# The 32x32 blocks of the delta rule's inverses: from ScalarE's copies to transfers within SBUF, and the decay bias moved into the exponential

## The chip, the cores and the metric

The kernel runs on one core of a Trainium2 chip. The metric is the device time of one execution in microseconds (us). Before the change it is 2154.05 us, the median of three runs (2153.97 to 2155.12). A core has five engines, each with an instruction queue of its own that is worked off in order: TensorE (PE, with weight loads listed as PEld), VectorE (DVE), ScalarE (ACT), GpSimd (POOL) and SyncE (SP), which in this kernel issues all DMA transfers.

## The reference, cut to what matters

One encoder layer: RMSNorm, one large input projection, a convolution branch, a gated delta-rule branch (8 heads, two directions), a merge, an output projection, a SwiGLU feed-forward layer and a per-layer embedding. Only the delta rule is touched. For each chunk of 64 positions and each head and direction it solves a unit lower triangular system:

```python
g = jnp.cumsum(g, axis=-1)
decay = jnp.exp(jnp.where(tri_incl, g[..., :, None] - g[..., None, :], -jnp.inf))
lower = jnp.where(tri_strict, jnp.einsum('bhncd,bhnsd->bhncs', k_beta, k) * decay, 0.0)
sol = lax.linalg.triangular_solve(lower, rhs, left_side=True, lower=True, unit_diagonal=True)
```

## The kernel before, in words

Everything is float32. The large products are made of three passes each (`mm3`: high times high, high times low, low times high, with parts rounded by ACT's cast and DVE's subtraction in `split`); their matmuls read 128x512 columns and appear in the profile as `ps<-big,w`. Below they are called fill, since they are what TensorE does beside the delta rule. The fill of the first half of the program is the input projection's columns, the gates, the embedding's projection and the convolution's output product.

The delta rule runs per group of two heads (`group(g)`, four groups), and in a group per head (`head(...)`). In `group`, section `d.np`, the decay matrix of a head is built for eight blocks of 128 positions: two rows of cumulated logs are broadcast from DRAM into `rf` and `rb`, each block gets its bias from `gneg`, a minimum picks the direction, and ACT takes the exponential. In section `d.inv` the 32x32 diagonal blocks of both heads (two directions, eight blocks of 128 with four 32-blocks each) are inverted together on DVE; the result is the tile `v`. In `head`, section `d.lev`, two transposes on DVE bring `v` into the tiles `rr` and `rt`; then for each half `q4` of the head two tiles `eu` and `et` (four blocks, two directions, 128x128 each) are filled with zeros by GpSimd, and sixteen 32x(4x32) pieces are copied onto their diagonals. Two levels of small float32 matmuls follow, each with a negation on ACT (`neg`) between its two products, which join 32-blocks to 64 and 64 to 128. After that come the values (`d.v`), the chain over the eight blocks in both directions (`d.chain`) and the output (`d.out`).

No order is written out by hand. The program is recorded as a list of operations (`Plan.add`), each with an engine, a cost and its buffers, and `Plan.order` puts them in order by a simulated run: each engine takes the ready operation of the lowest level (the delta rule -1.8, weight loads -3.0, fill 0.5 to 2.7) at the simulated time. The constants that the change touches belong to these costs (`SWITCH`, `DMA_LAT`, `DMA_RATE`, the extra cost in `act` and in `square_transpose`). So any change of a cost can move instructions everywhere in the program. The order on each engine is then fixed; on the chip each engine's queue waits at its head for semaphores. The tiles of the delta rule come from eleven buffers of line `d`; a raw weight block has four buffers, split weights six. All instructions are issued from helpers: L239 is a matmul, L244 a transpose on TensorE, L263 a plain copy or cast on ACT, L270 any other ACT function, L286 a DVE operation, L319 a zero fill, L335 a DMA.

Of the kernel before, what the change touches and what calls it, by code (L numbers as in the profile page):

```python
# [15 lines left out]
AF = mybir.ActivationFunctionType  # L16
# [124 lines left out]


TABLES = {AF.Exp: 0, AF.Sigmoid: 1, AF.Silu: 2, AF.Ln: 3}
SWITCH = 1.31
AGE = 4

COLD = 25.0

DMA_LAT, DMA_RATE = 1.6, 300000.0
HOLD = {"dve": 0.24, "act": 0, "pe": 0}  # L150


# [22 lines left out]
class Plan:  # L175
# [70 lines left out]
    def act(self, out, in_, func=AF.Copy, scale=1.0, bias=None, accum=None):  # L246
        cost = (0.051 if in_.buf.pool.space == PSUM else 0.093) + in_.n / 1200
        outs, ins, kw = [out], [in_], {}
        if isinstance(scale, View):
            ins.append(scale)  # L250
            cost += 0.093
        if isinstance(bias, View):
            ins.append(bias)
            cost += 0.093
        if accum is not None:
            outs.append(accum)
            cost += 0.125 if in_.buf.pool.space == PSUM else 0.1
        if out.p1 - out.p0 < P and out.buf.tag == "big" and out.n <= 256:
            cost += 0.125

        def go():
            if func == AF.Copy and accum is None and not isinstance(scale, View) and scale == 1.0:
                return self.nc.scalar.copy(out.ap(), in_.ap())  # L263
            if isinstance(scale, View) or scale != 1.0:
                kw["scale"] = scale.ap() if isinstance(scale, View) else scale
            if bias is not None:
                kw["bias"] = bias.ap() if isinstance(bias, View) else bias
            if accum is not None:
                kw["accum_out"] = accum.ap()
            return self.nc.scalar.activation(out.ap(), in_.ap(), func, **kw)  # L270

        self.add("act", go, outs, ins, cost, table=TABLES.get(func))
# [32 lines left out]

    def square_transpose(self, out, in_):
        self._vec("transpose", "dve", dict(out=out, in_=in_))
        self.ops[-1].cost += 0.14

    def recip(self, out, in_):  # L310
        self.add("dve", lambda: self.nc.vector.reciprocal(out=out.ap(), in_=in_.ap()), [out], [in_],
# [28 lines left out]
    def order(self):  # L340
# [59 lines left out]
        while len(done) < total:  # L400
# [65 lines left out]
            if e == "sp":  # L466
                free[e] = now + o.cost
                begin = max(dma_free, now + DMA_LAT)
                dma_free = begin + o.nbytes / DMA_RATE
                o.end = dma_free  # L470
            else:
                free[e] = o.end = now + o.cost
# [65 lines left out]
P = 128  # L538
# [17 lines left out]
def hs(h):  # L556
    return slice(h * HW, (h + 1) * HW)


def cs(j):  # L560
    return slice(j * P, (j + 1) * P)
# [45 lines left out]
def hybrid_block(tc, x, p, g_mix, w_in, conv_dw_w, conv_dw_b,  # L607
# [25 lines left out]
    def bank():  # L633
        return ps_.tile([P, HW], tag="ps", line="any", cap=bank_cap[0])
# [13 lines left out]
    def const(name, shape):  # L648
        return cp.tile(shape, tag=name)
# [23 lines left out]
    beta = const("beta", [P, 16, NJ])  # L673
    gdec = const("gdec", [P, 16, NJ])
    gneg = const("gneg", [P, 16, NJ])
    e_g = const("e_g", [P, 16, NJ])
    e_ng = const("e_ng", [P, 16, NJ])
    e_t = const("e_t", [P, 16, NJ])
# [154 lines left out]
    def logits():  # L833
        to(LV["logits"], "logits")
        wr = medium([P, KB, 32], line="wab")
        w2 = medium([P, KB, 64], F32R, line="wab2")
        pn.dma(wr, w_in[0, :, C_AB:C_AB + 32].rearrange("(k q) c -> q k c", q=P))
        split(w2[:, :, 0:32], w2[:, :, 32:64], wr)
        lg = large([64, T], line="lg")
        for h in range(2):  # L840
            ps = bank()[:64]
            for k in range(KB):
                for i in range(2):
                    pn.matmul(ps, w2[:, k], hT[i][k][:, hs(h)], k == 0 and i == 0, k == KB - 1 and i == 1)
            pn.act(lg[:, hs(h)], ps)
        ps = bank()
        for j in range(NJ):
            pn.matmul(ps[:, j * 32:(j + 1) * 32], lg[:, cs(j)], ident2, True, True)
        psv = ps[:, :NJ * 32].fold(NJ, 32).perm(1, 0)
        bc = tin.tile([P, 2, 16], tag="bc", bufs=1)  # L850
        pn.dma(bc[:, 0], a_log[0].rearrange("d h -> (d h)").partition_broadcast(P))
        pn.dma(bc[:, 1], dt_bias[0].rearrange("d h -> (d h)").partition_broadcast(P))
        g4 = medium([P, 4, 16, NJ], line="g4")
        ga, gu, ge, gl = [g4[:, i] for i in range(4)]
        pn.act(beta, psv[:, 16:32], AF.Sigmoid)
        pn.tt(ga, psv[:, 0:16], bc[:, 1, :, None].spread(16, NJ), ALU.add)
        pn.act(ge, ga, AF.Abs)
        pn.act(ge, ge, AF.Exp, scale=-1.0)
        pn.act(bc[:, 0], bc[:, 0], AF.Exp)

        pn.ts(gu, ge, 1.0, ALU.add)
        pn.act(gl, gu, AF.Ln)
        pn.stt(ge, gu, -1.0, ge, ALU.add, ALU.subtract)
        pn.recip(gu, gu)
        pn.tt(ge, ge, gu, ALU.mult)
        pn.tt(gl, gl, ge, ALU.subtract)
        pn.stt(gl, ga, 0.0, gl, ALU.max, ALU.add)
        pn.stt(gdec, gl, -1.0, bc[:, 0, :, None].spread(16, NJ), ALU.mult, ALU.mult)
        for dst, mf, mb in ((e_g, m_le, m_ge), (e_t, m_gt, m_lt), (e_l, ones, ones)):
            ps = bank()  # L870
            pn.matmul(ps[:, 0:64], mf, gdec[:, 0:8], True, True)
            pn.matmul(ps[:, 64:128], mb, gdec[:, 8:16], True, True)
            pn.act(dst, ps[:, :128].fold(16, NJ), AF.Exp)
            if dst is e_g:
                pn.act(gneg, ps[:, :128].fold(16, NJ), AF.Copy, scale=-1.0)
        pn.ts(e_ng, e_g, -1.0, ALU.mult)
        ps = bank()
        pn.transpose(ps[:, :P], gneg.at(0, [(1, P)]), ident)
        gr = medium([P, P], line="gr")
        pn.act(gr, ps[:, :P], AF.Copy, scale=-1.0)  # L880
        pn.dma(d_g, gr)
# [136 lines left out]
    def group(g):  # L1018
# [6 lines left out]
        for hh in range(2):  # L1025
# [23 lines left out]

            rf, rb = decay_row(hd), decay_row(8 + hd)  # L1050
            for j in range(NJ):
                pn.act(rf[:, cs(j)], rf[:, cs(j)], AF.Identity, bias=gneg[:, hd, j:j + 1])
            for j in range(NJ):
                pn.stt(rf[:, cs(j)], rb[:, cs(j)], gneg[:, 8 + hd, j:j + 1], rf[:, cs(j)], ALU.add, ALU.min)
            for q4 in range(2):
                ps = bank()
                for i in range(4):
# [2 lines left out]
                    pn.act(ps[:, cs(i)], ps[:, cs(i)], AF.Square, accum=ssq[:, hh, j:j + 1])  # L1060
            pn.ts(ssq[:, hh], ssq[:, hh], EPS, ALU.add)
            dec = rf
            for q4 in range(2):
                pn.act(dec[:, hs(q4)], dec[:, hs(q4)], AF.Exp)

            nt = slot([P, NJ, P])
            for q4 in range(2):
# [57 lines left out]
    def head(g, hh, v, N, kT, nrm, b_, zt, ssq):  # L1125
        hd = 2 * g + hh

        pn.sec = "d.lev"
        rr, rt = slot([P, 32, 2, 16]), slot([P, 32, 2, 16])
        pn.square_transpose(rr.at(0, [(32, 32), (1, 32)]), v)  # L1130
        pn.square_transpose(rt.at(0, [(32, 32), (1, 32)]), v.perm(1, 0))
        U = []
        for q4 in range(2):
            eu, et = slot([P, 4, 2, P]), slot([P, 4, 2, P])
            pn.fill(eu, 0.0)
            pn.fill(et, 0.0)
            u0 = hh * 8 + q4 * 4
            for r in range(4):
                q = slice(32 * r, 32 * r + 32)

                pn.act(eu[q, :, 0, q], rt[q].at(16 + u0, [(1, 4), (32, 32)]))
                pn.act(eu[q, :, 1, q], rr[q].at(u0, [(1, 4), (32, 32)]))
                pn.act(et[q, :, 0, q], rt[q].at(u0, [(1, 4), (32, 32)]))
                pn.act(et[q, :, 1, q], rr[q].at(16 + u0, [(1, 4), (32, 32)]))
            nt = N[:, q4 * 4:q4 * 4 + 4]
            ps = bank()
            for u in range(4):
                pn.matmul(ps[:, cs(u)], nt[:, u], pair32(et, u), True, True)

            w1 = neg(ps)  # L1150
            px = bank()
            for u in range(4):
                pn.matmul(px[:, cs(u)], w1[:, u], pair32(eu, u), True, True)

            for c in range(4):
                q, r = slice(32 * (c ^ 1), 32 * (c ^ 1) + 32), slice(32 * c, 32 * c + 32)
                pn.act(eu[q, :, c % 2, r], px[q].fold(4, P)[:, :, r])
            pn.square_transpose(et[32:64, :, 0, 0:32], eu[0:32, :, 1, 32:64])
            pn.square_transpose(et[64:96, :, 1, 96:128], eu[96:128, :, 0, 64:96])
            ps = bank()  # L1160
            for u in range(4):
                pn.matmul(ps[:, cs(u)], nt[:, u], pair64(et, u), True, True)
            w2 = neg(ps)
            px = bank()
            for u in range(4):
                pn.matmul(px[:, cs(u)], w2[:, u], pair64(eu, u), True, True)
            for c in range(2):
                q, r = slice(64 * (1 - c), 64 * (1 - c) + 64), slice(64 * c, 64 * c + 64)
                pn.act(eu[q, :, c, r], px[q].fold(4, P)[:, :, r])
            U.append(eu)  # L1170
# [602 lines left out]
```

## Time and profile before

| | |
|---|---|
| median of 3 runs | 2154.05 us |
| the profiled execution | 2155.1 us |
| its span, first to last instruction | 2153.4 us |
| mean granted TensorE clock | 0.992 |
| DMA issues on SP | 1003 |

The span has four stretches: a start up to 200 us, the delta rule with fill from about 200 to 1050 us, the passage to the output products from 1050 to 1300 us, and large products from there to the end. A row of the view by windows gives, for each stretch, the busy time of each engine with the number of instructions in brackets, then the granted TensorE clock, the mean share of the DMA engines and GB/s. A row of the groups gives line, engine, operation, output<-input, shape, count, busy time and mean duration in ns, and the idle time just before. A row of the view of waits says which engine waited for which operation: total, times, longest.

### The profile page before, as it was taken

The numbers are of one execution on the slowest core, as the hardware profiler recorded it, in microseconds if no ns is written. First come the engines' busy times: TensorE is split into PE (matmuls) and PEld (weight loads), VectorE is DVE, ScalarE is ACT, GpSimd is POOL, SyncE is SP. The second block draws the span as 40 slices with busy tenths as digits, with TensorE's granted clock in tenths as the row PEclk, the third lists the DMA queues.
The fourth block names the chain that finished last, engine by engine and source line by source line (L and its number), as shares of the span: only waits on it lengthen the run. The fifth ranks groups of instructions, "written<-read, shape, count | busy, mean of one in ns | idle before, by whom it ended". The sixth has DMA issues, their size and how long they took to land.

```text
span 2153.4 us, 29679 instructions
## 1 busy us (share of the span) xinstructions
PE 2102.0 (98%) x10434; PEld 1733.1 (80%) x10434; DVE 1602.6 (74%) x2621; ACT 1082.5 (50%) x2495; POOL 129.1 (6%) x203
## 2 busy tenths in 40 slices
PE   7999999999999999999999999999999999999998
PEld 5888788878888888888887788888888888888888
DVE  4478989869799899986846877886666667452676
ACT  6725665856675666479644344533333334121542
POOL 1000110012010110101000000000000000000000
PEclk9999999999999999999999999999999999999999
DMA  6333323522442324435567587332222228221253
GB/s 212 119 102 119 123 74 102 189 83 84 133 152 74 128 103 142 142 115 174 174 212 222 189 265 245 103 97 84 74 83 83 84 72 279 66 94 38 66 166 110
DMA packets 289077, 278.69 MB, mean 129 GB/s; under 512 B 17209, under 2 KB 217074, under 8 KB 288928
## 3 DMA queue, kind: packets, MB, share of 16 engines
q1 hardware_dynamic: 288928, 276.79, 40.2%
q8 instruction: 82, 1.34, 0.3%
q14 instruction: 67, 0.55, 0.1%
HBM read 198.02 MB, written 78.71 MB: 129 GB/s over the span
## 4 chain that ended last, share of the span: by engine, by line
PE 52%; DVE 3%; ACT 2%; issue 1%; DMA 0%; SPq 0%; DVEq 0%; POOLq 0%; POOL 0%; ACTq 0%
PE ps L239 52%; DVE big L286 2%; ACT big L263 1%; DVE mid L286 1%; DVE w L286 0%; PE ps L244 0%; DMA mid<-d 0%; ACT mid L270 0%; ACT big L270 0%; ACT m L270 0%; ACT mid L263 0%; ACT w L263 0%; SPq L335 0%; ACT z L270 0%; DVE lnb L286 0%
## 5 line engine op out<-in xcount | busy, mean ns | idle before, releaser
L239 PE MATMUL ps<-big,w 128*128 128x512 f32 (+1 forms) x7524 | 1841.4, 399 | 7.4 <-DVE w L286 5.8
L239 PEld LDWEIGHTS ps<-big,w 128*128 128x128 f32 x7524 | 1384.6, 189 | 315.8 <-DVE w L286 7.9
L286 DVE SCALAR_TENSOR_TENSOR big<-big,cw 128x1024 f32<-128x1024 f32 x336 | 433.3, 1295 | 16.4 <-ACT big L270 10.3
L263 ACT CAST w<-raw 128x512 fp32r<-128x512 f32 (+2 forms) x340 | 199.6, 590 | 367.2 <-PE ps L239 282.5
L286 DVE TENSOR_TENSOR w<-raw,w 128x512 fp32r<-128x512 f32 (+2 forms) x340 | 223.2, 662 | 114.0 <-ACT w L263 108.1
L263 ACT CAST w<-mid 128x512 fp32r<-128x512 f32 x125 | 77.4, 621 | 155.7 <-PE ps L239 129.3
L286 DVE TENSOR_TENSOR big<-ps,big 128x512 f32<-128x512 f32 (+1 forms) x132 | 89.7, 686 | 83.1 <-PE ps L239 75.9
L286 DVE TENSOR_TENSOR w<-mid,w 128x512 fp32r<-128x512 f32 x125 | 85.7, 687 | 79.8 <-ACT w L263 79.6
L286 DVE TENSOR_TENSOR big<-big 128x512 fp32r<-128x512 f32 (+2 forms) x159 | 107.4, 708 | 10.6 <-ACT big L263 10.2
L239 PE MATMUL ps<-big 128*128 128x128 f32 (+1 forms) x784 | 105.6, 282 | 8.7 <-ACT big L263 6.2
L239 PEld LDWEIGHTS ps<-big 128*128 128x128 f32 x784 | 100.0, 193 | 17.4 <-issue 9.2
L263 ACT COPY big<-big 32x128 f32<-32x128 f32 (+1 forms) x264 | 102.4, 441 | 15.5 <-DVE big L286 9.1
L263 ACT COPY big<-ps 32x128 f32<-32x128 f32 (+3 forms) x162 | 66.6, 412 | 71.9 <-PE ps L239 65.9
L263 ACT CAST big<-big 128x512 fp32r<-128x512 f32 x120 | 71.2, 619 | 44.3 <-DVE big L286 23.1
L244 PE MATMUL ps<-ident,big 128*128 128x128 f32 (+2 forms) x432 | 73.8, 286 | 10.4 <-DMA big<-in_x_dram 8.1
L270 ACT ACTIVATE mid<-mid 128x512 f32<-128x512 f32 (+2 forms) x87 | 50.6, 590 | 59.3 <-DMA mid<-d 31.0
L239 PEld LDWEIGHTS ps<-S,big 128*128 128x128 f32 x448 | 69.3, 190 | 13.0 <-DVE S L286 1.7
L239 PE MATMUL ps<-S,big 128*128 128x128 f32 x448 | 74.2, 276 | 2.0 <-DVE S L286 1.7
L239 PEld LDWEIGHTS ps<-big,m 128*128 128x128 f32 x512 | 63.8, 196 | 14.0 <-ACT m L270 12.0
L244 PEld LDWEIGHTS ps<-ident,big 128*128 128x128 f32 (+2 forms) x432 | 55.1, 149 | 22.7 <-issue 10.5
L239 PE MATMUL ps<-big,m 128*128 128x128 f32 x512 | 67.6, 283 | 4.6 <-ACT m L270 4.4
L270 ACT ACTIVATE big<-big 128x1024 f32<-128x1024 f32 (+2 forms) x80 | 56.8, 714 | 28.9 <-DVE big L286 24.1
(158 smaller groups left out, 1697.2 us busy)
## 6 DMA issues: line engine op xcount, KB each, us to landing
d<-mid SPq DMA_DIRECT2D x162, 256.0 KB, 2.3
raw<-in_w_in_dram SPq DMA_DIRECT2D x128, 256.0 KB, 3.1
mid<-d SPq DMA_DIRECT2D x120, 256.0 KB, 3.1
big<-d SPq DMA_DIRECT2D x92, 256.0 KB, 5.0
big<-dqkv SPq DMA_DIRECT2D x32, 512.0 KB, 4.1
raw<-in_w_gate_up_dram SPq DMA_DIRECT2D x50, 256.0 KB, 2.9
dqkv<-big SPq DMA_DIRECT2D x24, 512.0 KB, 2.6
mid<-in_w_gate_up_dram SPq DMA_DIRECT2D x46, 256.0 KB, 3.8
```

Of the source, the lines that this page charges most:

```text
L239: o = self.add("pe", lambda: self.nc.tensor.matmul(out.ap(), lhsT.ap(), rhs.ap(), start=start, stop=stop), [out], [lhsT, rhs], cost)
L244: self.add("pe", lambda: self.nc.tensor.transpose(out.ap(), in_.ap(), ident.ap()), [out], [in_, ident], 0.110)
L263: return self.nc.scalar.copy(out.ap(), in_.ap())
L270: return self.nc.scalar.activation(out.ap(), in_.ap(), func, **kw)
L286: return getattr(e, name)(**{k: v.ap() if isinstance(v, View) else v for k, v in kw.items()})
```

## The change

Three things change in what is computed where, and four planner costs with them.

1. In `d.lev` the sixteen ACT copies per half head become sixteen DMAs from `rr` and `rt` to `et` and `eu` (256 in all, 16 KB each); those of `et` now stand ahead of those of `eu`. For the source of each to be contiguous, `rr` and `rt` are laid out as (unit, column) and the two transposes write with a stride of 32 elements.
2. In `d.np` ACT's eight additions of `gneg` to `rf` per head go. The minimum uses the difference `gdif` of both directions' biases, computed once, and the forward bias is added inside the exponential, which is now eight ACT instructions of 128 columns per head instead of two of 512.
3. Planner: a table switch costs 1.41 instead of 1.31, a DMA holds the simulated transfer line at least 0.3, a short copy costs 0.025 more, a large square transpose 0.36 more.

```diff
-SWITCH = 1.31
+SWITCH = 1.41
...
-DMA_LAT, DMA_RATE = 1.6, 300000.0
+DMA_LAT, DMA_RATE, DMA_MIN = 1.6, 300000.0, 0.3
...
-            cost += 0.125
+            cost += 0.15
...
-        self.ops[-1].cost += 0.14
+        self.ops[-1].cost += 0.14 if out.n < T else 0.5
...
-                dma_free = begin + o.nbytes / DMA_RATE
+                dma_free = begin + max(o.nbytes / DMA_RATE, DMA_MIN)
...
+    gdif = const("gdif", [P, NH, NJ])
...
+        pn.tt(gdif, gneg[:, NH:], gneg[:, :NH], ALU.subtract)
...
-                pn.act(rf[:, cs(j)], rf[:, cs(j)], AF.Identity, bias=gneg[:, hd, j:j + 1])
-            for j in range(NJ):
-                pn.stt(rf[:, cs(j)], rb[:, cs(j)], gneg[:, 8 + hd, j:j + 1], rf[:, cs(j)], ALU.add, ALU.min)
+                pn.stt(rf[:, cs(j)], rb[:, cs(j)], gdif[:, hd, j:j + 1], rf[:, cs(j)], ALU.add, ALU.min)
...
-            for q4 in range(2):
-                pn.act(dec[:, hs(q4)], dec[:, hs(q4)], AF.Exp)
+            for j in range(NJ):
+                pn.act(dec[:, cs(j)], dec[:, cs(j)], AF.Exp, bias=gneg[:, hd, j:j + 1])
...
-        rr, rt = slot([P, 32, 2, 16]), slot([P, 32, 2, 16])
-        pn.square_transpose(rr.at(0, [(32, 32), (1, 32)]), v)
-        pn.square_transpose(rt.at(0, [(32, 32), (1, 32)]), v.perm(1, 0))
+
+        rr, rt = slot([P, 32, 32]), slot([P, 32, 32])
+        pn.square_transpose(rr.at(0, [(1, 32), (32, 32)]), v)
+        pn.square_transpose(rt.at(0, [(1, 32), (32, 32)]), v.perm(1, 0))
...
-            for r in range(4):
-                q = slice(32 * r, 32 * r + 32)
-
-                pn.act(eu[q, :, 0, q], rt[q].at(16 + u0, [(1, 4), (32, 32)]))
-                pn.act(eu[q, :, 1, q], rr[q].at(u0, [(1, 4), (32, 32)]))
-                pn.act(et[q, :, 0, q], rt[q].at(u0, [(1, 4), (32, 32)]))
-                pn.act(et[q, :, 1, q], rr[q].at(16 + u0, [(1, 4), (32, 32)]))
+            for dst, d, src, u in ((et, 0, rt, u0), (et, 1, rr, 16 + u0), (eu, 0, rt, 16 + u0), (eu, 1, rr, u0)):
+                for r in range(4):
+                    q = slice(32 * r, 32 * r + 32)
+                    pn.dma(dst[q, :, d, q], src[q, u:u + 4])
```

The planner makes a new order of the whole program from this. Two places show it, both in `d.lev` of the seventh head (the first of the last group). On ScalarE the old order has there, with `big<-big 32x4x32` the pieces of `eu` and `et`, `w<-raw` the casts of weights for the fill, and `m<-ps` the negations:

```order
L263 COPY big<-big 32x4x32 x11
L263 CAST w<-raw 128x512
L263 COPY big<-big 32x4x32 x9
L263 CAST w<-raw 128x512
L270 ACTIVATE m_8897<-ps 128x512
L263 COPY big<-big 32x4x32 x5
L263 COPY big<-ps 32x4x32 x4
L263 COPY big<-big 32x4x32 x7
L270 ACTIVATE m_8936<-ps 128x512
```

and the new one, from the last weights before the first negation to the second negation:

```order
L263 CAST w<-raw 128x256
L263 CAST big<-ps 128x512
L263 CAST w<-raw 128x256
L263 CAST big<-ps 128x512
L263 COPY mid<-ps 128x512
L270 ACTIVATE m_9042<-ps 128x512
L263 COPY mid<-ps 128x512
L263 COPY big<-ps 32x4x32 x4
L270 ACTIVATE m_9085<-ps 128x512
```

The 32 copies are gone from between the casts and negations, and work of the embedding's projection (`w<-raw 128x256`, `big<-ps 128x512`) stands in their place.

On SyncE the old order has at this head, from the last weight load ahead of it, loads and stores of whole tiles:

```order
L335 DMA raw<-in_w_in_dram 128x4x128 x2
L335 DMA big<-dqkv_6_5742 128x1024
L335 DMA d_8948<-mid 128x512
L335 DMA d_8953<-mid 128x512
L335 DMA m_9004<-d_8285 128x512
```

and the new one, where `big<-big 32x4x32` are the new transfers:

```order
L335 DMA raw<-in_w_pl_proj_dram 128x2x128
L335 DMA d_8934<-mid 128x512
L335 DMA big<-big 32x4x32 x24
L335 DMA raw<-in_w_pl_proj_dram 128x2x128 x2
L335 DMA d_9071<-mid 128x512
L335 DMA d_9076<-mid 128x512
L335 DMA raw<-in_w_pl_proj_dram 128x2x128 x2
L335 DMA big<-big 32x4x32 x8
L335 DMA big<-dqkv_6_5997 128x1024
```

Here 24 transfers stand between two weight loads. Over the whole program the 256 transfers lie in runs of 1 to 31 between weight loads, six of them of 21 or more. ScalarE's queue has 41 activation table loads instead of 36.

## The prediction

> **What bounds the kernel now.** I read the page's busy times first, then the view by windows, then TensorE's waits in the stretch that the change touches, and last the timeline at the largest of them.
>
> ```profile
> PE 2102.0 (98%) x10434; PEld 1733.1 (80%) x10434; DVE 1602.6 (74%) x2621; ACT 1082.5 (50%) x2495; POOL 129.1 (6%) x203
> ```
>
> The line holds for the whole span: TensorE is busy 98% of it, so all that any change on other engines can return is TensorE's idle time, 2153.4 - 2102.0 = 51.4 us, and time at a lowered clock. Where it lies, the windows tell:
>
> ```profile
> 0.00:200.00 200.00, 187.05 (x911) 149.97 (x912) 124.49 (x186) 118.03 (x248) 11.89 (x37) 0.98 0.43 141
> 200.00:1050.00 850.00, 827.74 (x4622) 697.65 (x4622) 744.84 (x1230) 560.37 (x1539) 106.68 (x153) 0.99 0.37 122
> 1050.00:1300.00 250.00, 244.13 (x1033) 194.98 (x1032) 172.73 (x276) 115.05 (x197) 1.39 (x1) 0.98 0.70 221
> 1300.00:2100.00 800.00, 799.83 (x3508) 647.73 (x3507) 525.51 (x846) 275.31 (x475) 4.69 (x5) 1.00 0.35 108
> ```
>
> The columns after the stretch are PE, PEld, DVE, ACT, POOL. From 1300 to 2100 us there is nothing to gain. In the delta rule's stretch, 200 to 1050 us, TensorE is idle for 850 - 827.7 = 22.3 us; DVE is busy 88% (744.8 of 850) and ACT 66%. So the change aims at the second busiest helper, not the busiest. What TensorE waits for in that stretch, largest first:
>
> ```profile
> PE ps L239 <- ACT big L263: 6.2, 4, 2.6
> PE ps L239 <- ACT m L270: 4.4, 8, 1.4
> PE ps L244 <- DVE m L286: 2.9, 5, 0.9
> ```
>
> The first row is the change's own place: products of `d.lev` that wait for copies into `et` and `eu`. The second is the negation in the same section. The timeline at the seventh head shows both:
>
> ```profile
> 912.02 3.21 DVE L286 STREAM_TRANSPOSE big<-big 128x1024 f32<-128x1024 f32 x2
> 913.34 0.43 ACT L263 COPY big<-big 32x128 f32<-32x128 f32 x1 [4.51 <-DVE big L286]
> 915.26 3.85 ACT L263 COPY big<-big 32x128 f32<-32x128 f32 x10 [1.49 <-DVE big L286]
> 919.13 0.62 ACT L263 CAST w<-raw 128x512 fp32r<-128x512 f32 x1
> 919.78 3.16 ACT L263 COPY big<-big 32x128 f32<-32x128 f32 x9
> 921.69 1.27 PE L239 MATMUL ps<-big 128*128 128x128 f32 x8 [2.54 <-ACT big L263]
> ```
>
> The transposes end at 915.23 (912.02 + 3.21); ACT copies, casts one block of weights, copies on, and the first product starts at 921.69, 6.46 us after the transposes. A cast of fill weights stands in line behind ten copies, so the fill is late too.
>
> ```profile
> 460.00:470.00 10.00, 7.35 (x37) 5.61 (x37) 4.47 (x4) 8.38 (x23) 0.00 (x0) 1.00 0.09 27
> 915.00:925.00 10.00, 6.84 (x31) 5.22 (x30) 8.65 (x9) 9.58 (x26) 0.00 (x0) 0.88 0.00 0
> 925.00:935.00 10.00, 8.65 (x42) 7.57 (x41) 9.69 (x10) 7.01 (x20) 0.00 (x0) 0.61 0.26 86
> ```
>
> ACT is busy 9.58 of 10 us there. The last number but two is the granted clock: 0.88 and 0.61 after 915, 1.00 at 460 although TensorE was idle there for 2.65 us as well. The loss is 10 x 0.12 + 10 x 0.39 = 5.1 us of full clock. The Trainium skill, "TensorE: Matmul & The Clock Gate", Part 1, says that the clock halves after an idle window of about 3.4 us; the trace agrees so far as 2.65 us of idle time left it at 1.00 and 3.16 us in one stretch did not. By that rule the 5.1 us go once the idle time is clearly under a window; without it they could stay, and the forecast below would be 2150.
>
> **The change part by part.** ScalarE first:
>
> ```profile
> L263 ACT COPY big<-big 32x128 f32<-32x128 f32 x256 | 93.3, 418 | 15.3 <-DVE big L286 9.1 <-POOL big L319 3.2 <-issue 1.6
> L270 ACT ACTIVATE big<-big,gneg 128x128 f32<-128x128 f32 x64 | 19.8, 392 | 0.1
> L270 ACT ACTIVATE big<-big 128x512 f32<-128x512 f32 x16 | 9.8, 623 | 0.1
> L270 ACT ACT_TABLE_LOAD x35 | 44.9, 1283 | 5.1 <-DVE big L286 4.5
> ```
>
> The 256 copies go: -93.3 us. The 64 additions of `gneg` go (-19.8), the 16 exponentials go (-9.8), and 64 exponentials with a bias on 128 columns come, which I price like the additions (+19.8; the trace has no such exponential, so between 9.8, were they no dearer together than the 16, and 64 x 0.623 = 39.9). Five more table loads cost 5 x 1.28 = 6.4. ScalarE loses 97 us, nearly all between 200 and 1050 us, where it was not the bound over the whole but in single places. DVE's minimum keeps its 64 instructions, and `gdif` is one instruction more, nothing.
>
> VectorE's transposes:
>
> ```profile
> L286 DVE STREAM_TRANSPOSE big<-big x2: 1230/1638/2045, 912.0 to 913.2; 128x1024 f32<-128x1024 f32 x2
> ```
>
> Of the two, the contiguous one (`rr`) took 1.23 us and the one that reads with a stride (`rt`) 2.05. Now both write with a stride, which the trace does not show. I take 2.05 for both, as for the strided read, the nearest row: eight times 0.82 = 6.6 us more on DVE. The ends are 0 and, if a strided write costs 0.82 on top of a strided read, 16 x 0.82 = 13.1. DVE is the busiest helper here, so this is not fully hidden; its convolution work stands behind the transposes, and the fill's weight halves too. With no cover at all it would cost TensorE 6.6; with DVE idle 12% of the time and TensorE short of 3% of it I count 2.
>
> SyncE and the transfers:
>
> ```profile
> L335 SPq DMA_DIRECT2D raw<-in_w_in_dram x94: 367/383/793, 200.2 to 1046.3; - x94
> d<-m SPq DMA_DIRECT2D x12, 256.0 KB, 2.0
> big<-dg SPq DMA_DIRECT2D x12, 512.0 KB, 5.7
> SPq L335 <- DVE w L286: 169.3, 47, 15.5
> ```
>
> An issue takes 0.383 us on SP, so 256 add 98 us to a queue that mostly waits (the last row: 169.3 us in the stretch, up to 15.5 at a time, only until raw weight buffers come free). A transfer within SBUF is not in the trace. The rows of issue to landing run from 2.0 us (a store) to 5.7 (a broadcast of 512 KB); these are 16 KB, so I take 2.0 and keep 5.7 for the range. In the new order at the seventh head one piece of `eu` and the eight of `et` follow the second transpose: the ninth issue starts 8 x 0.383 = 3.1 us after its end and lands at 3.1 + 2.0 = 5.1 us, against 6.46 with ScalarE. The first product can start 1.4 us earlier, and the rest of `eu` is needed only by the second product. With 5.7 us it would come 8.8 us after, 2.3 later than now.
>
> The sum on TensorE's path: each of the four waits of the first row shrinks by up to 1.4 us, 5.6 if all were that long; as they sum to 6.2 with one of 2.6, some are shorter, and I take 4.5. The clock loss goes, since what is left of the wait at 918 is about as long as that at 464, which cost no clock: 5.1. Negations stand no longer behind copies: half of 4.4, 2.2. Given back: 2 for DVE and 1 for weight loads that stand behind transfers in SP's queue. Net 4.5 + 5.1 + 2.2 - 2 - 1 = 8.8 us. The profiled execution takes 2155.1 us, of which 1.7 lie around the span; 2155.1 - 8.8 = 2146.3. The median of the runs, 2154.05, is 1.05 lower, so 2145.2 there, rounded to **2145**.
>
> **The rivals.** *More than that.* All of ScalarE's 97 us act: casts come early everywhere, and the new order leaves TensorE no idle time in the stretch. Then all 22.3 us and the clock's 5.1 go: 2154 - 27 = 2127 at best, and 2154 - 20 = 2134 with a quarter left. For it speaks that the new order has only fill casts around the negations; against it that about half of the 22.3 us (all but 6.2 and 4.4) is waits for operations that the change leaves as they are, on a DVE that gets slower.
>
> *Nothing that shows.* DVE at 88% is the bound behind ScalarE. The casts come earlier, but their low halves, the transposes and the convolution come from DVE, so the waits change their name from ACT to DVE. Of the 11.8 us only the clock's 5.1 stay, less 3 given back: 2152, within 4.3 us (0.2%, about what a measurement can tell from no change).
>
> *Slower, by SP's queue.* Its place is a run of transfers between two weight loads. A load of four weight tiles feeds 12 matmuls (three passes); at the rate of the last quoted window, 799.83 us for 3508 records, that is 12 x 0.228 = 2.7 us, and with two blocks ahead (the fill's cap) 5.5 us of cover. A run of more than 5.5 / 0.383 = 14 transfers outlasts it. The new order has six runs of 21 to 31, together 153, so 153 - 6 x 14 = 69 issues, 26 us of late weights, less the gain of 11.8: 2154 + 14 = 2168. Landings of 5.7 us instead of 2.0 lead the same way: eight heads with 2.3 us more at the first product are 18 us, less what remains of the gain. Against it: in the quoted wait row SP already sits up to 15.5 us between two loads because the buffers are full, so most of the runs may fall into such pauses. The Trainium skill, "DMA: Bandwidth & Descriptors", section "Rules for kernel authors", says of many small transfers to coalesce them, since "under 64 KB you're paying mostly overhead". By its fixed cost of about 2.0 us one after another, 256 transfers would be an estimated 512 us of waiting; whether it bites hangs on how many are in flight, and no run here shows it yet. The row of 2.0 us for 256 KB agrees with the fixed cost.
>
> *Not what it says.* The transfers replace the copies in every head, by the order, so this is ruled out; only the gain is open.
>
> **How the numbers follow.** Forecast, faster by 4.4 to 15 us: 0.43, at 2145. More, 2127 to 2139: 0.14. Nothing that shows, 2150 to 2158: 0.20. Slower, 2159 to 2175: 0.23, since two unknowns (landing and runs) lead there and the whole order is new. Faster is 0.43 + 0.14 = 0.57. For the range I leave out the lower half of "more" (0.06) and the upper part of "slower" (0.11): 2130 to 2164.
>
> **What would show it.** After the change the wait of TensorE for `ACT big L263` between 200 and 1050 us should be gone and one for `DMA big<-big` of under 3 us in total stand there; the clock between 900 and 950 us should stay at 1.00; ACT should be busy about 985 us, DVE about 1609; the transfers should land in 2.0 us. The step on the transposes is wrong if `rr` or `rt` takes other than 2.05 us. The forecast is wrong if waits of `ACT w` for `DMA raw` grow by over 10 us, or if TensorE's idle time turns up behind DVE instead.

## The result and the profile after

The changed kernel takes 2171.62 us (median of 4 runs, 2168.43 to 2173.65) against 2154.01 for the one before (4 runs): the ratio is 1.0081, 95% interval 1.0064 to 1.0098. It is slower by 17.6 us, and above the predicted range of 2130 to 2164. The profiled execution is the quickest of the four, with 2168.43 us and a span of 2166.7, 13.3 more than the span of before, so the profile shows three quarters of the loss.

The first line of the page, busy time and instructions by engine:

```profile
PE 2100.1 (97%) x10434; PEld 1737.2 (80%) x10434; DVE 1608.9 (74%) x2622; ACT 989.1 (46%) x2228; POOL 131.3 (6%) x203
```

ScalarE lost 93 us of work, VectorE gained 6.3, and TensorE has 66.6 us of idle time instead of 51.4. The windows say where (columns after the stretch: PE, PEld, DVE, ACT, POOL, granted clock):

```profile
200.00:1050.00 850.00, 815.47 (x4476) 688.00 (x4475) 716.42 (x1147) 434.05 (x1183) 102.30 (x145) 0.99 0.39 121
1050.00:1300.00 250.00, 240.13 (x1118) 196.60 (x1117) 193.52 (x331) 142.00 (x273) 7.55 (x9) 0.98 0.70 223
1300.00:2100.00 800.00, 800.00 (x3470) 645.79 (x3469) 523.35 (x838) 275.41 (x472) 4.03 (x4) 1.00 0.35 110
```

In the delta rule's stretch TensorE is idle for 34.5 us (22.3 before) and gets through 4476 matmuls instead of 4622; another 4.0 us of idle time come in the next stretch, where the end of the delta rule now lies, and nothing changes from 1300 on. What TensorE waits for between 200 and 1050 us (total, times, longest):

```profile
PE ps L239 <- DMA big<-big: 13.3, 9, 2.8
PE ps L239 <- DVE big L286: 5.6, 2, 4.2
PE ps L239 <- ACT big L270: 4.5, 2, 2.3
PE ps L239 <- issue: 3.7, 4, 2.5
PE ps L239 <- ACT big L263: 3.0, 1, 3.0
```

A wait for the transfers stands on top, more than twice as large as the wait for ScalarE's copies whose place it took (6.2 before; what is left of that name is a cast at 964). The timeline at the third head (the first of the second group), with start and length of each group and TensorE's waits in brackets:

```profile
450.18 4.11 DVE L286 STREAM_TRANSPOSE big<-big 128x1024 f32<-128x1024 f32 x2
...
452.34 3.25 SPq L335 DMA_DIRECT2D big<-big  x4
...
455.67 0.54 SPq L335 DMA_DIRECT2D raw<-in_w_in_dram  x1
456.27 18.05 SPq L335 DMA_DIRECT2D big<-big  x28
...
462.06 1.13 PE L239 MATMUL ps<-big 128*128 128x128 f32 x8 [1.95 <-DMA big<-big]
...
465.42 1.13 PE L239 MATMUL ps<-big,m 128*128 128x128 f32 x8 [0.83 <-DMA big<-big]
...
475.81 1.13 PE L239 MATMUL ps<-big,m 128*128 128x128 f32 x8 [1.67 <-DMA big<-big]
```

Twenty-eight issues take 18.05 us, one every 0.645. The trace's landing records put a transfer's end a median of 1.84 us after its issue starts (smallest 1.80). The two together give both products to a tenth: the seventh issue of the run starts at 456.27 + 6 x 0.645 = 460.14 and lands at 461.98, and the product starts at 462.06; the last one starts at 473.69 and lands at 475.53, and the last product waits until 475.81. SyncE, which only issues, has become what TensorE waits for. Here the first product starts 462.06 - 454.29 = 7.8 us after the transposes; at the same head before, with ScalarE, it was 467.01 - 461.42 = 5.6 us:

```profile
459.36 2.06 DVE L286 STREAM_TRANSPOSE big<-big 128x1024 f32<-128x1024 f32 x1
...
467.01 1.13 PE L239 MATMUL ps<-big 128*128 128x128 f32 x8 [2.60 <-ACT big L263]
```

The row of 13.3 us understates the transfers. The nine products that it counts start 0.09 to 0.28 us after the landing of a piece. Seven more products of `d.lev` start just as closely behind one, five of them after 0.20 us and two after 0.09, though the view names `issue`, `ACT big L270` or `ACT mid L263` for them; these waits are 9.3 us. By the landing records the pieces therefore cost TensorE 22.6 us of waiting.

The answer for this line between 457 and 474 us gives the issue by itself (duration min/median/max in ns), and the one below it the two transposes:

```profile
L335 SPq DMA_DIRECT2D big<-big x27: 585/599/608, 456.9 to 473.7; - x27
```

```profile
L286 DVE STREAM_TRANSPOSE big<-big x2: 2097/2144/2190, 450.2 to 452.1; 128x1024 f32<-128x1024 f32 x2
```

### The profile page after: what moved, and what is told of

Read it like the earlier page. It is cut to its first block, busy times and chain, and to the rows that moved or that the text cites. A ratio compares the mean times of both kernels' runs of the same rounds, so it can differ in the third digit from the quotient of the medians.

```text
span 2166.7 us, 29901 instructions
## 1 busy us (share of the span) xinstructions
PE 2100.1 (97%) x10434; PEld 1737.2 (80%) x10434; DVE 1608.9 (74%) x2622; ACT 989.1 (46%) x2228; POOL 131.3 (6%) x203
## 4 chain that ended last, share of the span: by engine, by line
PE 75%; DVE 10%; SPq 4%; ACT 3%; issue 3%; DMA 3%; POOL 0%; DVEq 0%; POOLq 0%; ACTq 0%
PE ps L239 74%; DVE big L286 7%; SPq L335 4%; DVE mid L286 2%; PE ps L244 2%; DVE w L286 1%; ACT big L270 1%; DMA raw<-in_w_in_dram 1%; DMA big<-big 1%; ACT big L263 1%; ACT ps L270 1%; ACT w L263 0%; ACT L270 0%; DMA dqkv<-big 0%; ACT m L270 0%
## 5 line engine op out<-in xcount | busy, mean ns | idle before, releaser
L263 ACT CAST w<-raw 128x512 fp32r<-128x512 f32 (+2 forms) x340 | 199.4, 589 | 404.1 <-PE ps L239 322.8
L263 ACT CAST w<-mid 128x512 fp32r<-128x512 f32 x125 | 77.4, 620 | 154.8 <-PE ps L239 123.3
L239 PEld LDWEIGHTS ps<-big 128*128 128x128 f32 x784 | 101.5, 194 | 21.5 <-issue 9.4
L263 ACT COPY big<-ps 128x512 f32<-128x512 f32 (+3 forms) x162 | 66.5, 411 | 78.3 <-PE ps L239 66.5
L263 ACT CAST big<-big 128x512 fp32r<-128x512 f32 x120 | 71.2, 619 | 41.3 <-DMA big<-d 20.9
L239 PEld LDWEIGHTS ps<-big,m 128*128 128x128 f32 x512 | 63.9, 196 | 22.6 <-issue 11.7
L286 DVE TENSOR_TENSOR big<-big,mid 128x512 f32<-128x512 f32 (+11 forms) x158 | 62.3, 394 | 13.7 <-ACT mid L270 8.8
L286 DVE STREAM_TRANSPOSE big<-big 32x128 f32<-32x128 f32 (+2 forms) x56 | 51.0, 922 | 26.9 <-ACT big L263 24.4
L270 ACT ACTIVATE mid<-mid 128x512 f32<-128x512 f32 (+2 forms) x87 | 50.2, 581 | 45.1 <-DVE mid L286 29.8
```

Of the source, the lines that this page charges most:

```text
L239: o = self.add("pe", lambda: self.nc.tensor.matmul(out.ap(), lhsT.ap(), rhs.ap(), start=start, stop=stop), [out], [lhsT, rhs], cost)
L286: return getattr(e, name)(**{k: v.ap() if isinstance(v, View) else v for k, v in kw.items()})
```

## The experiments

Three theories were set against each other. *Theory 1*: SyncE needs 0.60 us for an issue where the plan and the prediction had less, so the pieces come late. *Theory 2*: the new order that the planner makes from the new costs is worse by itself, whoever carries the pieces. *Theory 3*: the 64 small exponentials and the added table loads cost it. Ratios are to the kernel before in the same session (median 2154.3 to 2154.6). In the diffs, - is the changed kernel, except in the two where it is said to be the kernel before.

### One part at a time

The changed kernel without the edit of the decay bias:

```diff
-        pn.tt(gdif, gneg[:, NH:], gneg[:, :NH], ALU.subtract)
...
-                pn.stt(rf[:, cs(j)], rb[:, cs(j)], gdif[:, hd, j:j + 1], rf[:, cs(j)], ALU.add, ALU.min)
+                pn.act(rf[:, cs(j)], rf[:, cs(j)], AF.Identity, bias=gneg[:, hd, j:j + 1])
+            for j in range(NJ):
+                pn.stt(rf[:, cs(j)], rb[:, cs(j)], gneg[:, 8 + hd, j:j + 1], rf[:, cs(j)], ALU.add, ALU.min)
...
-            for j in range(NJ):
-                pn.act(dec[:, cs(j)], dec[:, cs(j)], AF.Exp, bias=gneg[:, hd, j:j + 1])
+            for q4 in range(2):
+                pn.act(dec[:, hs(q4)], dec[:, hs(q4)], AF.Exp)
```

> The changed kernel without the edit on the bias (ScalarE adds gneg to rf again, 16 exponentials of 512 columns). Theory 1 (SyncE needs 0.60 us for each transfer within SBUF, not 0.383, so sixteen pieces arrive over 10 us and TensorE waits for them): as slow as the changed kernel, 2165 to 2176 us, TensorE's wait for DMA big<-big 10 us or more. Theory 3 (the 64 small exponentials and their table loads cost the time): 2150 to 2158 us.

Measured: 2181.96 us, ratio 1.0128 (1.0114 to 1.0141). TensorE's first two waits between 200 and 1050 us are

```profile
PE ps L239 <- DMA big<-big: 13.2, 9, 2.8
PE ps L239 <- issue: 12.7, 6, 3.2
```

The loss is there, and larger, without the exponentials (28 us, where up to 22 were expected), so they cannot be its cause. The added table loads are only in part gone here (39, against 41 in the changed kernel and 36 before); two versions below with half of the pieces on GpSimd (2134.1 and 2128.1 us) keep the exponentials and all 41 and are faster than the kernel before, which settles Theory 3.

The kernel before with only the edit of the decay bias and the old planner's costs (- is the kernel before):

```diff
+        pn.tt(gdif, gneg[:, NH:], gneg[:, :NH], ALU.subtract)
...
-                pn.act(rf[:, cs(j)], rf[:, cs(j)], AF.Identity, bias=gneg[:, hd, j:j + 1])
-            for j in range(NJ):
-                pn.stt(rf[:, cs(j)], rb[:, cs(j)], gneg[:, 8 + hd, j:j + 1], rf[:, cs(j)], ALU.add, ALU.min)
+                pn.stt(rf[:, cs(j)], rb[:, cs(j)], gdif[:, hd, j:j + 1], rf[:, cs(j)], ALU.add, ALU.min)
...
-            for q4 in range(2):
-                pn.act(dec[:, hs(q4)], dec[:, hs(q4)], AF.Exp)
+            for j in range(NJ):
+                pn.act(dec[:, cs(j)], dec[:, cs(j)], AF.Exp, bias=gneg[:, hd, j:j + 1])
```

> The kernel before with the edit on the bias alone, copies by ScalarE, old planner costs. Theory 1: within 6 us of before (2148 to 2160 us), and ScalarE busy about 10 us less. Theory 3: 2165 us or more. Theory 2 (a new order of the whole program is what costs): anything from 2150 to 2175 us, since this order is new as well.

Measured: 2154.77 us, ratio 1.0001 (0.9992 to 1.0010). Alone it moves nothing that can be measured.

The kernel before with only the planner's new costs (- is the kernel before):

```diff
-SWITCH = 1.31
+SWITCH = 1.41
-DMA_LAT, DMA_RATE = 1.6, 300000.0
+DMA_LAT, DMA_RATE, DMA_MIN = 1.6, 300000.0, 0.3
-            cost += 0.125
+            cost += 0.15
-        self.ops[-1].cost += 0.14
+        self.ops[-1].cost += 0.14 if out.n < T else 0.5
-                dma_free = begin + o.nbytes / DMA_RATE
+                dma_free = begin + max(o.nbytes / DMA_RATE, DMA_MIN)
```

> The kernel before with the planner's new costs alone (table switch 1.41, short copy +0.025, large transpose +0.36, least transfer 0.3); the same work in another order. Theory 1: 2146 to 2160 us. Theory 2: 2165 us or more.

Measured: 2155.20 us, ratio 1.0002 (0.9993 to 1.0011). Its windows:

```profile
200.00:1050.00 850.00, 834.60 (x4577) 702.58 (x4576) 725.48 (x1175) 547.10 (x1478) 98.92 (x145) 1.00 0.37 122
1050.00:1300.00 250.00, 231.87 (x1063) 187.92 (x1063) 185.54 (x314) 133.55 (x258) 6.21 (x8) 0.96 0.67 212
```

An order from other costs moves idle time about (15.4 us in the first stretch instead of 22.3, 18.1 in the second instead of 5.9) and leaves the time where it was. This re-planning, at least, does not cost 18 us.

### The price that the planner has

The changed kernel, with the measured spacing of the transfers in the planner's table in place of 0.475 us. All 256 transfers stay on SyncE:

```diff
-                 0.475, nbytes)
+                 0.645 if nbytes == 16384 else 0.475, nbytes)
```

> The changed kernel with the planner told that a transfer within SBUF takes SyncE 0.645 us instead of 0.475. If the planner's wrong price is what makes TensorE stand (its queue has the products too early): 2150 to 2162 us, TensorE's wait for DMA big<-big under 5 us. If the arrival itself is too slow whatever the order: 2163 to 2176 us. Theory 2 has no forecast but that the time moves by some 10 us either way.

Measured: 2153.41 us, ratio 0.9993 (0.9985 to 1.0002): 18.2 us below the changed kernel, by one number in a table. At the same head its timeline reads

```profile
444.55 4.10 DVE L286 STREAM_TRANSPOSE big<-big 128x1024 f32<-128x1024 f32 x2
...
456.42 1.13 PE L239 MATMUL ps<-big 128*128 128x128 f32 x8 [0.16 <-DMA big<-big]
```

The first product starts 456.42 - 448.65 = 7.8 us after the transposes, just as late as in the changed kernel. But the planner now knows it and gives TensorE fill until then: it waits 0.16 us instead of 1.95. The row of waits for the transfers in the stretch comes to

```profile
PE ps L239 <- DMA big<-big: 2.2, 3, 1.7
```

Counted by the landings, as above, they are 3.3 us instead of 22.6: 19.3 less, where the time fell by 18.2. So the loss is the difference between the price in the plan and the price on the chip. The transfers' slowness itself can be covered. What this doesn't show is why the version gains nothing over the kernel before, with ScalarE 100 us freer.

### The same order, with the queue relieved

The changed kernel's own order of instructions on TensorE, with every second piece issued from another engine's queue (`nc.gpsimd` below; `nc.scalar` in the other version):

```diff
-        self.add("sp", lambda: self.nc.sync.dma_start(out=ap(out), in_=ap(in_)),
+        small = nbytes == 16384
+        self.n_small = getattr(self, "n_small", 0) + small
+        queue = self.nc.gpsimd if small and self.n_small % 2 else self.nc.sync
+        self.add("sp", lambda: queue.dma_start(out=ap(out), in_=ap(in_)),
```

> The changed kernel in exactly its own order, but every second transfer within SBUF is issued from ScalarE's queue instead of SyncE's. Theory 1 (SyncE's 0.60 us per issue is the limit): sixteen pieces take about 5.2 us instead of 10.3, TensorE's wait for them falls under 6 us, 2152 to 2164 us, unless ScalarE's own queue is held up by what its transfers wait for. Theory 2 (the order itself is bad, whoever issues): 2166 to 2176 us.

> The same with GpSimd's queue for every second transfer; GpSimd is nearly idle, and what its issue costs no run here shows. Theory 1: 2152 to 2164 us if it takes up to 0.65 us, no faster than the changed kernel if it takes more than 1.3 us. Theory 2: 2166 to 2176 us.

Measured: from ScalarE 2145.25 us, ratio 0.9954 (0.9942 to 0.9966); from GpSimd 2134.09, ratio 0.9905 (0.9892 to 0.9918). Both are below the 2152 to 2164 us that Theory 1 had. With GpSimd it is 37 us below the changed kernel, in the same order, with the same number of transfers. No wait for `DMA big<-big` is left on TensorE in either. The first line of the page with GpSimd (span 2134.0 us):

```profile
PE 2092.2 (98%) x10434; PEld 1732.4 (81%) x10434; DVE 1608.5 (75%) x2622; ACT 988.5 (46%) x2228; POOL 201.5 (9%) x331
```

TensorE's idle time is 41.8 us instead of 66.6. These 24.8 us, of which the waits for pieces were 22.6, are most of the 32.7 between the two spans; the other 7.9 are less busy time, at a mean granted clock of 0.995 instead of 0.991. This settles Theory 2: the order is not bad; it is 20 us better than the one before as soon as the pieces arrive when the plan has them. GpSimd's issues (duration min/median/max, ns):

```profile
L338 POOL DMA_DIRECT2D big<-big x128: 551/551/754, 222.3 to 1012.3; - x128
```

At the third head the two queues work side by side:

```profile
444.53 4.07 DVE L286 STREAM_TRANSPOSE big<-big 128x1024 f32<-128x1024 f32 x2
...
449.62 9.71 SPq L338 DMA_DIRECT2D big<-big  x15
...
453.08 4.89 POOL L338 DMA_DIRECT2D big<-big  x9
454.30 1.05 PE L239 MATMUL ps<-big 128*128 128x128 f32 x8
```

The product starts 454.30 - 448.60 = 5.7 us after the transposes, with no wait in brackets. ScalarE gains less as a helper; each issue is again 0.60 us there (median 602 ns), on an engine that has copies and negations behind it.

All 256 from GpSimd, in the same order:

```diff
-        self.add("sp", lambda: self.nc.sync.dma_start(out=ap(out), in_=ap(in_)),
+        queue = self.nc.gpsimd if nbytes == 16384 else self.nc.sync
+        self.add("sp", lambda: queue.dma_start(out=ap(out), in_=ap(in_)),
```

> The changed kernel in exactly its own order with all 256 transfers within SBUF issued from GpSimd's queue (0.55 us each in the run with half of them there). SyncE has then only loads and stores. If what costs the time is that the pieces themselves come late (sixteen need 8.8 us instead of 10.3): 2160 to 2172 us with a wait of TensorE for DMA big<-big of 8 us or more. If it is that weight loads and other loads stand behind the pieces in SyncE's queue: 2132 to 2150 us.

Measured: 2162.67 us, ratio 1.0037 (1.0023 to 1.0050), 9 us below the changed kernel, and the wait is back:

```profile
PE ps L239 <- DMA big<-big: 12.7, 5, 4.3
```

SyncE's weight loads have no pieces ahead of them here, yet nearly half of the loss stays (8.1 of 17.6 us), as expected for pieces that come late. GpSimd's queue alone is too slow for this order too, though it has no weight loads to issue. It is not the issue rate alone: GpSimd issues every 0.54 us (19 in 10.28 at the third head) instead of every 0.645, but its zero fills of 0.98 us stand between the pieces, and the first product of that head starts 9.3 us after the transposes instead of 7.8. The 9 us between the two kernels are not settled: loads no longer stand behind transfers, and the spacing is smaller.

### Size or number

Each piece moves one of its four units, 4 KB instead of 16 (three quarters of the inverses' diagonal blocks stay zero, so this kernel does not compute the layer):

```diff
-        self.add("sp", lambda: self.nc.sync.dma_start(out=ap(out), in_=ap(in_)),
+        small = nbytes == 16384
+
+        def part(x):
+            return x[:, 0:1] if small else x
+
+        self.add("sp", lambda: self.nc.sync.dma_start(out=ap(part(out)), in_=ap(part(in_))),
```

> The changed kernel in exactly its own order, but each transfer moves one unit of 32x32 instead of four (three quarters of the inverses' diagonal blocks stay zero). If the 0.60 us go with the size of the piece: an issue under 0.45 us and 2150 to 2162 us by theory 1. If they are a price per transfer: an issue of 0.60 us still and 2166 to 2176 us. Theory 2: 2166 to 2176 us in either case.

Measured: 2164.24 us (2159.45 to 2169.60), ratio 1.0046 (1.0032 to 1.0059), and the issue

```profile
L340 SPq DMA_DIRECT2D big<-big x256: 507/588/1565, 219.8 to 1043.1; - x128
```

A quarter of the data saves 11 ns of 599 at the issue and 0.10 us of 1.84 at the landing. The price goes by the transfer. The time still fell by 7.4 us, just under the 2166 that was expected for a price per transfer, and the runs do not show why. Smaller transfers would not have saved the change; fewer would, as the next run shows.

### Fewer transfers, and versions that use what was found

With the price of 0.645 us: the pieces of `et` by ScalarE's copies, only those of `eu` by transfers.

```diff
-                    pn.dma(dst[q, :, d, q], src[q, u:u + 4])
+                    if dst is et:
+                        pn.act(dst[q, :, d, q], src[q, u:u + 4])
+                    else:
+                        pn.dma(dst[q, :, d, q], src[q, u:u + 4])
```

> The changed kernel with the pieces of et copied by ScalarE as before and those of eu moved by transfers, the planner told 0.645 us for these. Theory 1: half the issues (83 us of SyncE), the pieces that the first product needs come from ScalarE in about 8 x 0.36 us, the others have time until the second product: 2142 to 2153 us, at or below the kernel before. Theory 2 has no forecast: 2145 to 2175 us.

Measured: 2137.50 us, ratio 0.9923 (0.9910 to 0.9936). Half the transfers on SyncE, and 16.5 us below the kernel before; 2142 to 2153 had been expected.

Every second piece from GpSimd without the edit of the decay bias, to see what that edit is worth with the queue out of the way (the first diff of this section and this one together):

```diff
+        small = nbytes == 16384
+        self.n_small = getattr(self, "n_small", 0) + small
+        queue = self.nc.gpsimd if small and self.n_small % 2 else self.nc.sync
```

> The kernel with the transfers alone (bias added by ScalarE as before), every second transfer issued from GpSimd. Theory 1: the time of its order without late pieces; if the edit on the bias is worth nothing, 2130 to 2140 us as with the bias in the exponential, if it is worth what lies between the two kernels with all transfers on SyncE (10 us), 2140 to 2150 us.

Measured: 2145.63 us, ratio 0.9959 (0.9946 to 0.9971). The same with the edit is 11.5 us quicker, as the changed kernel is 10.3 quicker than the transfers alone; on the kernel before, the edit brought nothing. Each of these pairs differs in its order too, so whether the edit or the order brings the 10 us stays open.

Half of the pieces from GpSimd, and the planner told so (the issue 0.645 us, on GpSimd's own time, its landing 0.7 us later):

```diff
+        eng = "pool" if small and self.n_small % 2 else "sp"
+        queue = self.nc.gpsimd if eng == "pool" else self.nc.sync
+        self.add(eng, lambda: queue.dma_start(out=ap(out), in_=ap(in_)),
...
+                 0.645 if small else 0.475, nbytes)
...
-            if e == "sp":
+            if e == "sp" or o.nbytes:
...
-                o.end = dma_free
+                o.end = dma_free + (0.7 if e == "pool" else 0)
```

> Every second transfer on GpSimd's queue, and the planner knows it (0.645 us of the issuing engine for each). Theory 1: no late pieces and an order made for them, 2125 to 2140 us, below both kernels. If only the order by chance made the run with half on GpSimd fast: 2140 to 2160 us.

and the split of `et` and `eu`, with the transfers of `eu` from GpSimd alone, priced in the planner in the same way:

```diff
+        eng = "pool" if small else "sp"
+        queue = self.nc.gpsimd if small else self.nc.sync
...
+                    if dst is et:
+                        pn.act(dst[q, :, d, q], src[q, u:u + 4])
+                    else:
+                        pn.dma(dst[q, :, d, q], src[q, u:u + 4])
```

> The pieces of et by ScalarE's copies, those of eu by transfers from GpSimd's queue, priced in the planner; SyncE has no piece at all. Theory 1: 2128 to 2142 us, like the two split kernels; not clearly better, since neither had waits for transfers left.

Measured: 2128.08 us (2127.02 to 2129.55), ratio 0.9875 (0.9862 to 0.9889), and 2130.78, ratio 0.9886 (0.9872 to 0.9899). The first is the quickest version found, 26 us below the kernel before. Its window of the delta rule:

```profile
200.00:1050.00 850.00, 843.35 (x4733) 717.75 (x4732) 757.52 (x1236) 477.14 (x1290) 177.07 (x281) 1.00 0.42 132
```

TensorE's idle time there is 6.7 us, against 22.3 before and 34.5 after, at a clock of 1.00.

## Why the prediction was wrong

**The step that failed** is "An issue takes 0.383 us on SP". The figure came from the nearest row, weight loads from device memory; a piece of 32 partitions within SBUF takes 0.60, and 0.645 from one issue to the next. With that in the same sum, the ninth piece lands 8 x 0.645 + 1.84 = 7.0 us after the transposes, where the prediction had 5.1 and ScalarE's copies took 6.46. At the seventh head, where the prediction reckoned it, the product starts 951.21 - 943.96 = 7.25 us after them. So the first product was to come 1.4 us earlier than before and comes 0.8 later there, and 2.2 later at the third head.

**A second fault of the same step**: "the rest of `eu` is needed only by the second product" took the remaining pieces as covered. Thirty-two pieces take 32 x 0.645 = 20.6 us of SyncE's time, and the product at 475.81 in the third head waits for the last of them, 21.5 us after the transposes. The prediction counted 98 us of issues on "a queue that mostly waits" and did not ask how long one head's 32 take in a row. By the measured spacing the 98 us are 256 x 0.645 = 165, and in seven of the eight heads a product of TensorE stands until the last of the 32 pieces has landed and starts within 0.25 us of it.

**The planner** was not in the prediction's argument. The plan had 0.475 us for an issue. TensorE's queue is in order, so a product that the plan puts too early stops the fill behind it: nine such waits by the view, 13.3 us, and sixteen by the landings, 22.6. That the loss lies in this gap is shown twice, by closing it in the plan (2153.4) and on the chip (2134.1).

**The clock** did not return its 5.1 us. From 900 to 950 it is at 1.00 now, as the prediction said; the head has moved to 940, and its first product waits only 0.38 us. But new waits take the clock down elsewhere, as at 540 (a product of the fourth head waits 2.82 us for its last piece), 960 and 1050:

```profile
540.00:550.00 10.00, 9.45 (x44) 8.34 (x45) 5.16 (x6) 2.81 (x8) 0.00 (x0) 0.68 0.72 238
960.00:970.00 10.00, 2.80 (x10) 1.56 (x9) 7.34 (x9) 2.50 (x6) 0.00 (x0) 0.82 0.54 146
1050.00:1060.00 10.00, 5.49 (x24) 4.92 (x23) 5.86 (x11) 3.97 (x9) 0.55 (x1) 0.75 0.96 302
```

Summed as the prediction did it, the rows from 530 to 550, 960 to 980 and 1050 to 1070 lose 10.3 us of full clock, twice the 5.1 of before. The reason given for the term was weak besides: the wait at 464, which cost no clock, was 2.60 us long and the one at 919, which did, 2.54, so the length of one wait does not tell the two apart.

**Weight loads behind transfers**, the mechanism of the rival "slower, by SP's queue", are seen behind the seventh head's run of 24:

```profile
961.67 0.40 ACT L263 CAST w<-raw 128x256 fp32r<-128x256 f32 x1 [3.04 <-DMA raw<-in_w_pl_proj_dram]
...
964.14 0.98 PE L239 MATMUL ps<-big,w 128*128 128x512 f32 x2 [3.02 <-ACT big L263]
```

A cast waits 3.04 us for weights and TensorE 3.02 for that chain; in the run with all pieces on GpSimd's queue TensorE has no such wait at this head. Over the stretch up to 1060 us, ScalarE's casts wait 12.5 us for weights and waited 12.4 before, far from the 10 us of growth that the prediction named as a sign. The rival's band (2159 to 2175) held the result, with the right queue; its price was not. It had 26 us of late weights or landings of 5.7 us; what decided was the issue of the pieces themselves, and they land in 1.84. That the band fits is luck: neither of the costs it was built from is the one that came.

**What held.** The transposes take 2.10 and 2.19 us, forecast 2.05 each, and VectorE as a whole gained 6.3 us where 6.6 were forecast. ScalarE is busy 989 us (985), VectorE 1608.9 (1609). A transfer lands in 1.84 us (2.0). The wait for ScalarE's copies is gone. The rival "more than that", 2127 to 2139, is what the change comes to once its queue is relieved: 2134.1 in the same order, 2128.1 with the plan right. Its chance was 0.14, for a reason that then didn't bind: VectorE at 89% (757.52 of 850) still left TensorE only 6.7 us of idle time.

The Trainium skill, "DMA: Bandwidth & Descriptors", "Rules for kernel authors", quoted ahead, was the better guide than the row: many small transfers pay an overhead apiece. The quarter-size run agrees, with 1.74 us to landing for 4 KB against 1.84 for 16. But the landings overlap; the issues on one queue did not. The Trainium skill, "DMA: Bandwidth & Descriptors", "Issuing engines are not separate DMA queues", says that starting DMAs on several engines only saves the time that a sequencer takes to start them, and that this is usually small beside the DMA itself. Here it was not small: an issue took 0.60 us of the 1.84 to landing, and taking half of the issues off SyncE brought the kernel from 2171.6 to 2134.1 us.

## What to carry to other kernels

Price a transfer's issue by its own form, not by the nearest other transfer, and multiply it by the number that must go in a row: a queue that is idle over the whole kernel can be the bound for 20 us at the place that counts. Where a planner sets the order, a changed kind of work needs its measured price in the plan before the change is judged; one number was worth 18 us here. The many small transfers did best here on two queues, one of them that of an engine with little else to do.

## What the runs showed of the hardware

The issue of a 16 KB transfer within SBUF occupies SyncE for 0.60 us, ScalarE for 0.60 and GpSimd for 0.55, against 0.38 for a 256 KB weight load on SyncE; the small transfer is the dearer one to issue. A transpose that writes with a stride takes 2.10 us, about what one that reads with a stride took before (2.05), and one that does both takes 2.19: the costs of the two strides do not add up, where the prediction had an upper end of 0.82 us more for that.
